# The output projection of a hybrid block: from eight products of halves to seven, with sums of weights made by DMA and by GpSimd

## The chip, the cores and the metric

The kernel runs on one core of a Trainium2 chip. The metric is the device time of one execution in microseconds (us). A core has a matrix engine (TensorE, here PE, with its weight loads shown apart as PEld), VectorE (DVE), ScalarE (ACT), GpSimd (POOL), and SyncE (SP), which only issues DMAs here. Matmuls write into PSUM, which is used as eight banks of 128x512 fp32; everything else is in SBUF.

## The reference

One block over 512 tokens of 1024 features, all in fp32; what matters here is its end:

```python
ya = einsum(ba * conv(ca * xa) * silu(za), w_a_out)          # short convolution branch
yb = einsum(sigmoid(o) * rmsnorm(mlstm(q, k, v, gates)) * silu(zb), w_b_out)   # 2048 -> 1024
merged = sigmoid(ga) * ya + sigmoid(gb) * yb
x = x + einsum('bsd,de->bse', merged, w_o)                   # 1024 -> 1024: the output projection
gate = sigmoid(einsum('bsd,de->bse', rmsnorm(x, g_ple), w_ple_gate))
x = x + gate * (p @ w_ple)
return rmsnorm(x, g_final)
```

## The kernel before

**Products.** Every fp32 product is made of three matmuls on rounded parts (`mm3`, lines 215 to 219): high by high (L217), high by low (L218), low by high (L219). So each operand is cut in two: ACT copies the high part (`whi`, L164) and DVE subtracts it from the original to get the low part (`wlo`, L165). The function `cut` (L221 to L228) does the same with left factors.

**Weights.** A weight block is 512 rows by 512 columns, in a tile `wraw` of 128x4x512 that an SP DMA fills (`load_raw`; four such tiles). It is an *operand* in the list `operands`, used in that order. Its two halves (rows 0 to 255 and 256 to 511, each a tile of 128x1024) are split one at a time by `split_half`; the second half of operand 115 is named `wlo1151`. The split tiles are double-buffered. After the low part of a half, sums that a later operand needs are made in place in another `wraw` tile: on DVE (L169), or by a GpSimd DMA that adds as it writes (L171), 256 or 512 KB each.

**Order of work.** The order on PE, ACT, DVE and POOL is that of the code; nothing is rescheduled. `step` is called after each 12 or 24 matmuls, and calls `tick` (L200), which in this order advances the follow-up work of the step before (`fresh`), splits one weight half of the next operand, and advances the generators in `active` (left factors, loads). So each engine's queue holds what belongs to the last group of matmuls, then a weight half, then left factors.

**Seven products.** `strassen` (L305) multiplies a 2 by 2 arrangement of halves in seven products (a variant of Strassen's scheme), with sums of weight blocks and of left factors as operands. For w_b_out it has two groups (2048 rows), so fourteen *units*, numbered 0 to 13, of 24 matmuls each (two token tiles of four row blocks by three matmuls), with left factors `l0` to `l13` made by `left_heads` (L1045 on) from the tiles `yf`. Its sums are b12 + b22 on DVE for units 7 and 9 and accumulating DMAs for the others. Results go through `sink_heads`: multiply by the gate (`sgx` or `sgb`), add to the merged tile `m`, and, when a pair of token tiles is done, transpose it on PE (`turn_half`, L1095, eight transposes into two banks `pth`) and cut it into the two parts `mg`.

**Output projection.** It is done plainly: two column halves of w_o, each with two row halves and four token tiles, so 8 products of 24 matmuls (operands 114 to 117). The loop at L1179 does the first column half in the order of the transposed quarters; `block_tm` does the second. `add_residual` (L1162) adds a finished bank to x, which lies in `xr`, and squares it on ACT for the norm. Then `turn_to` (L1123) transposes the new x, scales it by g_ple and cuts it into `h2`, the left factor of the w_ple_gate product (operands 118 to 121). `load_end` issues the loads of x, of p @ w_ple (`ple`, computed at the start and kept in DRAM) and of g_final on POOL's queue.

## Time and profile before

| | before |
|---|---|
| median of 3 runs (lowest to highest) | 864.36 us (864.03 to 864.46) |
| profiled execution | 863.96 us, span 862.2 us, mean granted PE clock 0.997 |
| PE busy | 849.0 us, 98%, 4658 instructions |
| PEld | 735.8 us, 85% |
| DVE | 630.4 us, 73% |
| ACT | 483.9 us, 56% |
| POOL | 218.0 us, 25% |

The span runs from the first to the last instruction of the profiled execution; the time beside it has in addition what lies around it, 1.8 us. Busy time is that in which an instruction of the engine runs; matmuls overlap one another, so a busy PE isn't necessarily one at its peak. A row of the listing gives its start in us, its duration, the engine, line and operation, output and inputs by name, their shape, and in brackets the idle time before it with what ended that. In the table by stretch the columns are the stretch, its length, and then the busy time with the count of instructions for PE, PEld, DVE, ACT and POOL, after them the granted clock, the DMA share and GB/s.

### The profile page before, as it was taken

How to read it: one execution, taken by the hardware profiler on the slowest of the kernel's cores; microseconds unless marked ns; L12 is line 12 of the kernel's file. 1: busy time of each engine (PE TensorE's matmuls, PEld its weight loads, DVE VectorE, ACT ScalarE, POOL GpSimd, SP SyncE). 2: the span in 40 equal slices, each digit the busy share in tenths (PEclk: the TensorE clock that was granted, in tenths of full speed). 3: DMA queues.
4: the chain of work that ended last, by engine and by line, in shares of the span. 5: the costliest groups of instructions: out<-in, count | busy, mean ns of one | idle time of the engine just before them, and what ended most of it. 6: DMA issues, size and time to landing. Idle time of an engine off the chain costs nothing.

```text
span 862.2 us, 12152 instructions
## 1 busy us (share of the span) xinstructions
PE 849.0 (98%) x4658; PEld 735.8 (85%) x4658; DVE 630.4 (73%) x813; ACT 483.9 (56%) x702; POOL 218.0 (25%) x221
## 2 busy tenths in 40 slices
PE   9999999999999999999999999999999999999996
PEld 7888888787889988878788999999998888888885
DVE  5786667966767576778568679897986778964465
ACT  7467655657755566565675555545453256634343
POOL 5103222113224322211214323333410212130031
PEclk9999999999999999999999999999999999999998
DMA  9749669589968998775999599899997487884002
GB/s 311 265 135 187 156 133 222 184 235 254 256 135 199 240 224 181 182 183 201 260 243 226 109 243 152 205 175 187 182 346 285 100 196 192 224 319 151 1 1 97
DMA packets 100138, 167.58 MB, mean 194 GB/s; under 512 B 5420, under 2 KB 45920, under 8 KB 98800
## 3 DMA queue, kind: packets, MB, share of 16 engines
q0 software_dynamic: 38672, 70.86, 42.3%
q1 hardware_dynamic: 58544, 90.97, 32.2%
q10 hardware_dynamic: 2864, 4.98, 1.6%
q8 instruction: 36, 0.59, 0.3%
q14 instruction: 22, 0.18, 0.1%
HBM read 150.01 MB, written 16.78 MB: 193 GB/s over the span
## 4 chain that ended last, share of the span: by engine, by line
PE 83%; issue 6%; DVE 4%; DMA 4%; ACT 3%; ACTq 0%; POOL 0%; SPq 0%; POOLq 0%; DVEq 0%
PE mm L218 25%; PE mm L217 25%; PE mm L219 25%; DMA wraw<-in_w_in 2%; DVE wlo L165 1%; PE pv L217 1%; PE pv L218 1%; PE pv L219 1%; ACT whi L164 1%; DMA xin<-in_x 1%; DMA z_d<-c 1%; PE sc L219 1%; PE sc L218 1%; PE sc L217 1%; DVE wraw L169 1%
## 5 line engine op out<-in xcount | busy, mean ns | idle before, releaser
L165 DVE TENSOR_TENSOR wlo<-wraw,whi 128x1024 fp32r<-128x1024 f32 x238 | 298.2, 1256 | 123.0 <-ACT whi L164 121.9
L164 ACT ACTIVATE whi<-wraw 128x1024 fp32r<-128x1024 f32 x240 | 250.8, 1054 | 105.2 <-PE mm L219 45.3
L171 POOL DMA_DIRECT2D wraw<-in_w_in x112 | 136.7, 1416 | 310.0 <-DVE wlo L165 227.1
L333 ACT ACTIVATE s<-mm 128x512 f32<-128x512 f32 x84 | 50.2, 598 | 99.9 <-PE mm L219 97.8
L217 PE MATMUL mm<-whi,hs 128*128 128x512 f32 x256 | 99.9, 390 | 0.0
L218 PE MATMUL mm<-wlo,hs 128*128 128x512 f32 x256 | 99.8, 390 | 0.0
L219 PE MATMUL mm<-whi,hs 128*128 128x512 f32 x256 | 99.7, 389 | 0.0
L217 PE MATMUL mm<-hn_hi,whi 128*128 128x256 f32 (+1 forms) x304 | 93.4, 307 | 0.0
L219 PE MATMUL mm<-hn_hi,wlo 128*128 128x256 f32 (+1 forms) x304 | 93.0, 306 | 0.0
L218 PE MATMUL mm<-hn_lo,whi 128*128 128x256 f32 (+1 forms) x304 | 92.9, 306 | 0.0
L217 PE MATMUL mm<-hs,whi 128*128 128x256 f32 x320 | 90.9, 284 | 0.0
L218 PE MATMUL mm<-hs,whi 128*128 128x256 f32 x320 | 90.5, 283 | 0.0
L219 PE MATMUL mm<-hs,wlo 128*128 128x256 f32 x320 | 90.5, 283 | 0.0
L218 PE MATMUL mm<-wlo,hn_hi 128*128 128x512 f32 x192 | 75.9, 396 | 3.1 <-DVE wlo L165 2.8
L217 PE MATMUL mm<-whi,hn_hi 128*128 128x512 f32 x192 | 75.6, 394 | 0.0
L219 PE MATMUL mm<-whi,hn_lo 128*128 128x512 f32 x192 | 74.9, 390 | 0.0
L218 PEld LDWEIGHTS mm<-hs,whi 128*128 128x128 f32 x320 | 61.4, 192 | 0.0
L217 PEld LDWEIGHTS mm<-hs,whi 128*128 128x128 f32 x320 | 61.4, 192 | 0.0
L219 PEld LDWEIGHTS mm<-hs,wlo 128*128 128x128 f32 x320 | 61.4, 192 | 0.0
L219 PEld LDWEIGHTS mm<-hn_hi,wlo 128*128 128x128 f32 x304 | 58.1, 191 | 2.8 <-POOL wlo L165 0.3
L218 PEld LDWEIGHTS mm<-hn_lo,whi 128*128 128x128 f32 x304 | 58.1, 191 | 2.4
L217 PEld LDWEIGHTS mm<-hn_hi,whi 128*128 128x128 f32 x304 | 58.1, 191 | 2.3
(306 smaller groups left out, 1673.9 us busy)
## 6 DMA issues: line engine op xcount, KB each, us to landing
wraw<-in_w_in SPq DMA_DIRECT2D x32, 1024.0 KB, 5.6
wraw<-in_w_in POOLq DMA_DIRECT2D x52, 512.0 KB, 7.9
wraw<-in_w_in SPq DMA_DIRECT2D x48, 512.0 KB, 5.3
wraw<-in_w_in POOLq DMA_DIRECT2D x60, 256.0 KB, 5.8
wraw<-in_w_b_out SPq DMA_DIRECT2D x7, 1024.0 KB, 6.2
wraw<-in_w_b_out POOLq DMA_DIRECT2D x12, 512.0 KB, 6.6
yt_d<-yc POOLq DMA_DIRECT2D x4, 1024.0 KB, 4.9
wraw<-in_w_a_out SPq DMA_DIRECT2D x4, 1024.0 KB, 6.1
```

What stands on the lines that cost most here:

```text
L164: act.activation(hi, t, AF.Copy)
L165: (e_lo or dve).tensor_tensor(lo, t, hi.bitcast(F32), ALU.subtract)
L169: eng.tensor_tensor(raws[to][:, ks, :], raws[to][:, ks, :], raws[c][:, ks, :], ALU.add)
L171: nc.gpsimd.dma_start(raws[to][:, ks, cs], src[:, ks, :], accum_op=ALU.add)
L217: pe.matmul(ps, lhsT=a[0], rhs=b[0], start=first, stop=False, **kw)
L218: pe.matmul(ps, lhsT=a[0], rhs=b[1], start=False, stop=False, **kw)
L219: pe.matmul(ps, lhsT=a[1], rhs=b[0], start=False, stop=last, **kw)
L333: act.activation(to[i], src, AF.Copy, scale=scale)
```

## The change

The w_o product becomes a seven-product scheme with one group. Its operands are o11, a sum, o21, the next sum, o22, o12 and the last sum. The tile `sums` begins as one more SP load of o11 (rows 512 on, columns 0 to 511), and three pairs of accumulating DMAs on POOL's queue bring it from one sum to the next; a fourth pair adds o22 into o12's tile for its own turn. No left over products are stored: each finished bank, or pair of banks, is added to or subtracted from x at once (`add_residual(row, n, op, src, last)`), and where that was the last part the square and the transposes follow. Banks go on accumulating over products.

The left factors are quarters of the merged tile (256 tokens by 512 features) and sums of them, made by `lefts_1` and `lefts_2` during the last units of the w_b product and by `lefts_3` during the new one. Names: f21, f1 and f11 are plain quarters and sums in fp32, in the place of `yf0` and in two temporaries; `la`, `lb`, `lc`, `ls` hold the cut factors (a11 and s1, s2 and a12, a22, s4 and s3). `at_once=True` lets the sixth w_b task run its sink one step sooner, and the transposes of quarters are issued by those generators. `low_on_pool` puts the low part of the second half of operands 118 (o22) and 119 (o12) on POOL. In the w_b product, the sums b12 + b22 (two pairs of halves) go from DVE to POOL.

After it, x is held with its token tiles in another order (`xs`), `turn_to` works on 256 tokens by 512 features, so `h2` is cut in pieces of 128x256, `ple` is read into the place of `m`, and the first column half of the w_ple_gate product goes over its quarters in the order (0, tokens 2, 3), (1, tokens 2, 3), (1, tokens 0, 1), (0, tokens 0, 1).

The core of the diff:

```diff
-            7: [(b12, b22, 0, dve)], 8: [(b11, b21, 0, None)], 9: [(b12, b22, 1, dve), (b11, b21, 1, None)]}
+            7: [(b12, b22, 0, pool)], 8: [(b11, b21, 0, None)], 9: [(b11, b21, 1, None), (b12, b22, 1, pool)]}
...
+    o11, sums, o21, o22, o12 = (chunk(w_o_v, k, [(n * CW, CW)]) for k, n in ((HC, 0), (HC, 0), (0, 0), (0, 1), (HC, 1)))
+    begun = {sums: o12}
+    first_o = len(operands)
+    operands.extend([(o11, []), (sums, [(sums, o22, None)]), (o21, [(o12, o22, None)]), (sums, [(sums, o21, None)]),
+                     (o22, []), (o12, []), (sums, [])])
+    low_on_pool = {(first_o + i, 1) for i in (4, 5)}
...
-        (e_lo or dve).tensor_tensor(lo, t, hi.bitcast(F32), ALU.subtract)
+        eng = e_lo or (pool if (i, h) in low_on_pool else dve)
+        eng.tensor_tensor(lo, t, hi.bitcast(F32), ALU.subtract)
...
+    def lefts_1():
+        q = quarter_turned(0, 1)
+        yield
+        for ks, pt in q:
+            act.activation(f21[:, ks, :], pt, AF.Copy)
+        q = quarter_turned(0, 0)
+        yield
+        for ks, pt in q:
+            dve.tensor_tensor(f1[:, ks, :], pt, f21[:, ks, :], ALU.subtract)
...
+        cut_quarter(o_a22, q)
+        yield
+        cut(*o_s1, f1)
+
+    def lefts_2():
+        q = quarter_turned(1, 1)
+        yield
+        cut_quarter(o_a11, q)
+        for ks, pt in q:
+            f11.append((ks, temp("c", "f11")))
+            act.activation(f11[-1][1].rearrange("p (f s) -> p f s", f=2), pt, AF.Copy)
+
+    def lefts_3():
+        for ks, f in f11:
+            dve.tensor_tensor(f1[:, ks, :], f1[:, ks, :], f.rearrange("p (f s) -> p f s", f=2), ALU.add)
+        act.activation(o_s2[0], f1, AF.Copy, scale=-1.0)
+        yield
+        dve.scalar_tensor_tensor(o_s2[1], f1, -1.0, o_s2[0].bitcast(F32), ALU.mult, ALU.subtract)
+        q = quarter_turned(1, 0)
+        yield
+        cut_quarter(o_a12, q)
+        for ks, f in f11:
+            pool.tensor_tensor(f21[:, ks, :], f.rearrange("p (f s) -> p f s", f=2), f21[:, ks, :], ALU.subtract)
+        yield
+        for ks, pt in q:
+            dve.tensor_tensor(f1[:, ks, :], f1[:, ks, :], pt, ALU.subtract)
+        yield
+        cut(*o_s4, f1)
+        yield
+        act.activation(o_s3[0], f21, AF.Copy)
+        pool.tensor_tensor(o_s3[1], f21, o_s3[0].bitcast(F32), ALU.subtract)
...
-    strassen(units, sink_heads, groups=2)
+    strassen(units, sink_heads, groups=2, at_once=True)
...
+    for left, banks, tag, row, n, op, last in (
+            (o_a11, acc, order[0], 1, 0, ALU.add, False),
+            (o_s1, cc, order[1], 2, 1, ALU.subtract, False),
+            (o_a12, bb, "x", 1, 0, ALU.add, True),
+            (o_s2, acc, None, 1, 1, ALU.subtract, False),
+            (o_s4, cc, None, 1, 1, ALU.subtract, True),
+            (o_s3, acc, None, 2, 1, ALU.subtract, True),
+            (o_a22, acc, None, 2, 0, ALU.add, True)):
+        w = next_operand()
+        post = add_residual(row, n, op, banks, last)
+        for i in range(2):
...
+            step(post(i))
```

**DVE, last unit of the w_b product.** Between the second low part of unit 12's weights (`wlo1121`) and that of unit 13's (`wlo1131`), before:

```order
L165 TENSOR_TENSOR wlo1121_6992<-wraw61_6171,whi1121_6991 128x1024
L337 TENSOR_TENSOR c_7024<-s_7022,v_6762 128x512
L165 TENSOR_TENSOR wlo1130_7027<-wraw62_6237,whi1130_7026 128x1024
L1029 SCALAR_TENSOR_TENSOR l13_6997<-yf3_6185,l13_6997 128x1024
L225 TENSOR_TENSOR mg1_6495<-pth_7000,mg0_6494 128x2x256
L225 TENSOR_TENSOR mg1_6495<-pth_7001,mg0_6494 128x2x256
L1111 TENSOR_TENSOR sgx0_6345<-sgx0_6345,c_6989 128x512
L1112 TENSOR_TENSOR m_4210<-m_4210,sgx0_6345 128x512
L165 TENSOR_TENSOR wlo1131_7050<-wraw62_6237,whi1131_7049 128x1024
```

and after:

```order
L184 TENSOR_TENSOR wlo1121_6993<-wraw61_6171,whi1121_6992 128x1024
L356 TENSOR_TENSOR c_7029<-s_7027,v_6755 128x512
L1188 TENSOR_TENSOR sgx1_6350<-sgx1_6350,c_7029 128x512
L1189 TENSOR_TENSOR m_4210<-m_4210,sgx1_6350 128x512
L184 TENSOR_TENSOR wlo1130_7034<-wraw62_6240,whi1130_7033 128x1024
L1050 SCALAR_TENSOR_TENSOR l13_6998<-yf3_6188,l13_6998 128x1024
L1149 TENSOR_TENSOR yf0_6185<-pth_7005,yf0_6185 128x512
L1149 TENSOR_TENSOR yf0_6185<-pth_7006,yf0_6185 128x512
L244 TENSOR_TENSOR lc_7040<-pth_7005,lc_7040 128x512
L244 TENSOR_TENSOR lc_7040<-pth_7006,lc_7040 128x512
L184 TENSOR_TENSOR wlo1131_7058<-wraw62_6240,whi1131_7057 128x1024
```

The merge into `m` that stood behind `l13` now stands ahead of it as one of two pairs, and in the place of the two `mg` rows stand the two rows of f1 and the two low parts of a22 (`lc`).

**DVE, middle of the output projection.** From the second low part of one operand over the following ones; before, operand 115, the second of four:

```order
L165 TENSOR_TENSOR wlo1151_7163<-wraw70_6951,whi1151_7162 128x1024
L1165 TENSOR_TENSOR xr_7113<-xr_7113,mm_7124 128x512
L225 TENSOR_TENSOR mg1_6495<-pth_7184,mg0_6494 128x2x256
L225 TENSOR_TENSOR mg1_6495<-pth_7185,mg0_6494 128x2x256
L1165 TENSOR_TENSOR xr_7113<-xr_7113,mm_7149 128x512
L165 TENSOR_TENSOR wlo1160_7244<-wraw71_6995,whi1160_7243 128x1024
L165 TENSOR_TENSOR wlo1161_7261<-wraw71_6995,whi1161_7260 128x1024
L1165 TENSOR_TENSOR xr_7113<-xr_7113,mm_7213 128x512
L1165 TENSOR_TENSOR xr_7113<-xr_7113,mm_7230 128x512
```

and after, operand 116, the third of seven, with product 4's weights (`wlo1170`, `wlo1171`) behind it:

```order
L184 TENSOR_TENSOR wlo1161_7237<-wraw71_6996,whi1161_7236 128x1024
L1178 TENSOR_TENSOR yf0_6185<-yf0_6185,pth_7185 128x512
L1178 TENSOR_TENSOR yf0_6185<-yf0_6185,pth_7186 128x512
L1258 TENSOR_TENSOR xr_7128<-xr_7128,mm_7222 128x512
L184 TENSOR_TENSOR wlo1170_7260<-wraw70_6940,whi1170_7259 128x1024
L244 TENSOR_TENSOR ls_7127<-yf0_6185,ls_7127 128x1024
L1258 TENSOR_TENSOR xr_7128<-xr_7128,mmb_7245 128x512
L184 TENSOR_TENSOR wlo1171_7285<-wraw70_6940,whi1171_7284 128x1024
L1258 TENSOR_TENSOR xr_7128<-xr_7128,mmb_7268 128x512
```

The two `mg` rows are gone, and the rows of sums and cuts of left factors (`yf0`, `ls`) and one more add from a bank to `xr` stand there.

**POOL, the same stage.** Before, its whole queue from the last gate loads to the first use of the norm (a count at the end of a row says that so many like it follow one another):

```order
L1154 DMA xr_7113<-in_x 128x512 x8
L1159 DMA ple_7115<-ple_d_92 128x1024 x4
L1160 DMA gfin_7114<-in_g_final 128x1024
L1200 TENSOR_TENSOR etmp1_7120<-etmp0_7119,mhalf_84 128x4
L1224 TENSOR_TENSOR xg_7443<-xr_7113,gfin_7114 128x512 x4
```

and after, from the sums of f21 to the last load:

```order
L1175 TENSOR_TENSOR yf0_6185<-f11_7095,yf0_6185 128x512
L1175 TENSOR_TENSOR yf0_6185<-f11_7097,yf0_6185 128x512
L158 DMA wraw73_7117<-in_w_o 128x2x512
L158 DMA wraw70_6940<-in_w_o 128x2x512
L1223 DMA ple_7264<-ple_d_92 128x1024
L158 DMA wraw70_6940<-in_w_o 128x2x512
L1223 DMA ple_7264<-ple_d_92 128x1024
L1183 TENSOR_TENSOR ls_7127<-yf0_6185,ls_7127 128x1024
L1223 DMA ple_7264<-ple_d_92 128x1024
L184 TENSOR_TENSOR wlo1181_7326<-wraw72_7061,whi1181_7325 128x1024
L1223 DMA ple_7264<-ple_d_92 128x1024
L1226 DMA gfin_7129<-in_g_final 128x1024
```

Between the loads now stand two sums of quarters, the summing DMAs of w_o, s3's low part and the two low parts of weights (`wlo1181`, `wlo1191`).

## The prediction

> **What bounds the kernel now.** I read, in this order, the page's busy times, the list of what TensorE (PE) waited for, the busy time by stretch, and then each engine's rows in order of time.

> ```profile
> span 862.2 us, 12152 instructions
> PE 849.0 (98%) x4658; PEld 735.8 (85%) x4658; DVE 630.4 (73%) x813; ACT 483.9 (56%) x702; POOL 218.0 (25%) x221
> PE mm L218 <- DVE wlo L165: 2.8, 6, 0.8
> 740.00:766.80 26.80, 26.80 (x128) 22.22 (x127) 26.29 (x31) 14.23 (x18) 7.60 (x15) 1.00 0.72 242
> 766.80:808.00 41.20, 41.20 (x196) 34.35 (x195) 16.10 (x19) 14.61 (x26) 0.47 (x1) 1.00 0.46 168
> 757.16 0.42 PE L218 MATMUL mm<-wlo,l 128*128 128x512 f32 x1
> 757.42 0.40 PE L219 MATMUL mm<-whi,l 128*128 128x512 f32 x1
> 749.39 0.87 PE pth L1102 x8
> ```

> PE is the bound: it waits 2.8 us in all for weights. But from 740.0 to 766.8 VectorE (DVE, third busy figure) works 26.29 of 26.80 us, and only in the output's projection (766.8 to 808) 16.10 of 41.20. So the projection has room; the last units of the product ahead of it have none.

> ```profile
> 746.70 0.60 ACT L333 ACTIVATE s<-mm 128x512 f32<-128x512 f32 x1 [3.02 <-PE mm L219]
> 747.19 1.05 ACT L164 ACTIVATE whi<-wraw 128x1024 fp32r<-128x1024 f32 x1
> 748.14 1.05 ACT L1028 ACTIVATE l<-yf 128x1024 fp32r<-128x1024 f32 x1
> 746.18 1.22 DVE L165 TENSOR_TENSOR wlo<-wraw,whi 128x1024 fp32r<-128x1024 f32 x1
> 747.32 1.22 DVE L1029 SCALAR_TENSOR_TENSOR l<-yf,l 128x1024 fp32r<-128x1024 f32 x1
> 753.28 1.28 DVE L225 TENSOR_TENSOR mg<-pth,mg 128x512 fp32r<-128x512 f32 x2
> 755.80 1.22 DVE L165 TENSOR_TENSOR wlo<-wraw,whi 128x1024 fp32r<-128x1024 f32 x1
> 742.39 0.69 DVE L1111 TENSOR_TENSOR sgb<-sgb,c 128x512 f32<-128x512 f32 x1
> 743.11 0.69 DVE L1112 TENSOR_TENSOR m<-m,sgb 128x512 f32<-128x512 f32 x1
> 743.72 1.22 DVE L165 TENSOR_TENSOR wlo<-wraw,whi 128x1024 fp32r<-128x1024 f32 x1
> 770.35 0.69 DVE L1165 TENSOR_TENSOR xr<-xr,mm 128x512 f32<-128x512 f32 x1 [3.61 <-PE mm L219]
> 771.07 0.63 ACT L1167 ACTIVATE esq<-xr 128x512 f32<-128x512 f32 x1 [7.31 <-DVE xr L1165]
> 771.70 1.07 ACT L224 ACTIVATE mg<-pth 128x512 fp32r<-128x512 f32 x2
> ```

> Prices, as steps from one start to the next: DVE 1.14 for 1024 columns (1.22 until its reader may start), 0.60 for 512 (0.69; 0.72 where the next row needs the result: 742.39 to 743.11); ScalarE (ACT) 0.95 (1.05), 0.50 (0.60), 0.63 for a square; 0.04 to hand over to another engine (770.35 + 0.69 to 771.07). PE: 757.16 to 757.42 holds a wait; an undisturbed step is (749.39 − 683.04 − 0.87) / 288 = 0.227, since 24 stretches of 12 matmuls and one set of 8 transposes lie between the row below and that of 749.39.

> ```profile
> 683.04 0.39 PE L217 MATMUL mm<-whi,l 128*128 128x512 f32 x1
> ```

> **The gain.** One product of halves less is 24 matmuls: 24 × 0.227 = 5.44 us. The eight sets of transposes stay eight.

> **The new waits.** In the new loop PE needs a fresh weight half every 5.44 us, 6.31 where a set of transposes (0.87) comes between. Each second half passes ACT (high part), then DVE or GpSimd (low part), in queues that also hold the adds from the banks and the left factors. What counts is the chain from the end of one late low part to the end of the next; PE waits for what it has over 5.44 or 6.31. GpSimd's part needs its own rows:

> ```profile
> 18.35 2.40 POOL L165 TENSOR_TENSOR wlo<-wraw,whi 128x1024 fp32r<-128x1024 f32 x1 [2.18 <-ACT whi L164]
> 19.20 2.07 DVE L228 SCALAR_TENSOR_TENSOR hn_lo<-pt,prm,hn_hi 128x512 fp32r<-128x512 f32 x3 [1.01 <-ACT hn_hi L227]
> 22.79 0.19 DVE L631 TENSOR_TENSOR wg<-wg_raw,wg 128x32 fp32r<-128x32 f32 x1
> 22.90 2.45 POOL L165 TENSOR_TENSOR wlo<-wraw,whi 128x1024 fp32r<-128x1024 f32 x1 [2.16 <-ACT whi L164]
> 23.10 2.30 DVE L631 TENSOR_TENSOR wg<-wg_raw,wg 128x32 fp32r<-128x32 f32 x1
> 829.61 1.29 POOL L1224 TENSOR_TENSOR xg<-xr,gfin 128x512 f32<-128x512 f32 x1 [1.36 <-DVE xr L1215]
> 834.74 3.44 DVE L165 TENSOR_TENSOR wlo<-wraw,whi 128x1024 fp32r<-128x1024 f32 x2
> 834.90 2.20 POOL L1224 TENSOR_TENSOR xg<-xr,gfin 128x512 f32<-128x512 f32 x1 [1.35 <-DVE xr L1215]
> L171 POOL DMA_DIRECT2D wraw<-in_w_b_out x12 | 14.5, 1215 | 68.9 <-DVE wlo L165 68.9
> L1159 POOL DMA_DIRECT2D ple<-ple_d x4 | 2.1, 534 | 1.3 <-DMA xr<-in_x 1.0 <-issue 0.3
> ```

> A GpSimd sum of 1024 columns takes 2.42. DVE rows with both inputs in SBUF stop for it (0.19 becomes 2.30 at 23.10), rows that read a bank don't (0.69 each at 19.20), and GpSimd stops for DVE's (1.29 becomes 2.20). I take it that the two take turns whole. [...]

> (a) The four weight sums (two pairs of halves) leave DVE: 4 × 1.14 = 4.56 us of DVE are freed where PE did not wait, so nothing is gained. But l7's low part, which followed one sum on DVE, now stands behind both turns of GpSimd's first pair: laid end to end, the first turn ends 0.16 before unit 7's predecessor is half done, then come a weight's low part (1.14), the second turn (2.35) and l7's own 1.22 = 4.71, while PE has 12 matmuls and wants it at the third of unit 7: 0.16 + 2.72 + 0.45 = 3.3. Late by 1.4.
> (b) Last unit: its second low part stood 9.62 us behind the row of 746.18 (755.80) and was just in time. Ahead of it now: one more pair sgx and m (0.72 + 0.60), two bank reads for f1 in the place of the two mg rows, and lc's two low parts (1.20), which wait for ACT (0.16 for its copy of a bank that DVE must have read first, 0.35 for the high part queued behind the copies): 0.72 + 0.60 + 1.20 + 0.51 = 3.0. Two more sets of transposes give PE 1.74. Late by 1.3.
> (c) Product 1: 1.14 low part, 1.14 s1's, 1.14 first half, 0.60 + 0.73 a11's, 0.50 copy, 1.09 high, = 6.34: 0.9 over 5.44.
> (d) Product 2: 1.14, 0.72 + 0.60 merge, 1.14, 0.60 + 0.73 sums of f1, 0.95 s2's high, 1.09 = 6.97: 0.65 over 6.31.
> (e) Product 3: 1.14, 1.14 s2's low, 0.60 add, 1.14, 1.20 a12's, 0.60 add = 5.82, and 0.92 behind GpSimd's first half of f21: 1.3 over 5.44.
> (f) Product 4: 1.14, 1.20 f1, 0.60 add, 1.14, 1.14 s4's low, 0.73 add, 0.63 square, 1.09 = 7.67: 2.2 over 5.44.
> (g) Product 5, low part on GpSimd: 0.04, issue of a summing DMA 1.20, ple's 0.53, s3's low 2.35, DVE's turn 1.14, 2.42 = 7.68: 1.35 over 6.31.
> (h) Product 6, again on GpSimd: 1.14, four cuts of h2 1.76 with the wait for ACT between them, 0.73 add, 0.63 square, 1.09, 2.42 = 7.77: 2.3 over 5.44.
> (i) Product 7 is in time (its chain has 5.0 of 6.31). First half of the next weights: 1.14, h2 1.77, 0.72, 0.63, 1.09, 1.22 = 6.57 against 2.72 + 0.87 + 1.59 (seven matmuls): 1.4. (j) Second: 0.73, 0.63, 1.09, 1.14, h2 with ACT 1.24, 1.09, 1.22, less 0.08 that the ends overlap = 7.06: 0.75 over 6.31.

> Sum: 1.4 + 1.3 + 0.9 + 0.65 + 1.3 + 2.2 + 1.35 + 2.3 + 1.4 + 0.75 = 13.55. Net 13.55 − 5.44 = +8.1.

> The unknown price is the h2 cut of 128x256 on DVE and ACT:

> ```profile
> 791.45 1.41 DVE L228 SCALAR_TENSOR_TENSOR h<-ptk,prm,h 128x512 fp32r<-128x512 f32 x2 [1.75 <-ACT h L227]
> 93.59 0.42 DVE L864 SCALAR_TENSOR_TENSOR pp<-sc,e 128x256 f32<-128x256 f32 x1
> wraw<-in_w_b_out POOLq DMA_DIRECT2D x12, 512.0 KB, 6.6
> xr<-in_x POOLq DMA_DIRECT2D x8, 256.0 KB, 5.4
> ```

> Between 0.33 (93.59 to the next start) and 0.70 (half of the 1.41 for two of 512) for one; I take 0.38, the row of 256 columns with 0.05 more for a bank as input. The four in each of (h), (i) and (j) move the sum by −0.6 to +3.8. Transfers: eight summing DMAs of 512 KB on GpSimd's queue and one more load on SP's are new. Product 4's first half is the tightest: the issue follows product 2's first low part (1.20), 6.6 to land, while its high part comes 7.2 later but its low part only 13; so up to 5 us of lateness stays hidden. Summing DMAs that queue behind GpSimd's sums start up to 2.4 later, nine ahead of use, and SP's next load waits for the same sums, with twenty to go: nothing. The second pair of x pieces goes behind a summing DMA (1.20 + 0.53 + 5.4 after product 2's first low part) and is wanted 8.5 after it: hidden by 1.4. ple, now read into m's place, is wanted 40 us on. DVE's own 3% and the hand-over (0.03 to 0.06) move the sum by −2 to +1.5, since they enter ten chains.

> **Rivals.** First, GpSimd runs beside DVE: then (a) is nothing, (e) loses 0.92, (g) 0.65 and (h) 1.45, since GpSimd waits for no turn and DVE starts (h) sooner: 9.1 of waits, +3.7, 867.6 us. The row of 23.10 speaks against it. Second, on the other side, the change does what it removes and nothing is late, because queued engines run further ahead than I let them: 863.96 − 5.44 = 858.5 us. It decides where the ten chains stay under 5.44 or 6.31; for it speaks that 766.8 to 808 shows DVE at 39% and that PE waited only 2.8 us before; against it the row of 757.16, where DVE was already just in time, and (f), which is over by 2.2 without GpSimd at all. Third, waits of about 5.4 in all cancel the gain: every chain would have to be 0.8 shorter: 864 us. Fourth, PE's clock falls in the pauses, or summing DMAs land over 5 us late: above 875.9. The granted clock is 1.00 beside the 0.8 us wait and lower only at the end:

> ```profile
> 150.00:210.00 60.00, 58.44 (x260) 46.74 (x259) 45.62 (x49) 38.86 (x54) 10.14 (x11) 1.00 0.76 225
> 840.00:862.20 22.20, 14.01 (x85) 12.41 (x83) 12.40 (x33) 7.32 (x17) 2.19 (x4) 0.88 0.25 94
> ```

> No row has a 2 us pause amid work; a fall would add from nothing to a few us. [...]

> **How the numbers follow.** The profiled execution took 863.96 us (span 862.2), 0.4 under the median of 864.36. 863.96 + 8.1 = 872.1. Chances: this case 0.62, first rival 0.20, second 0.08, third 0.04, fourth 0.06. Range: below, the first rival with chains 1.3 shorter in sum, 866.3; above, the long h2 cut, 875.9. It leaves out the second, third and fourth and a little of the others' edges. A difference of 0.2% (1.7 us) is about what can be told from none: faster 0.08, same 0.05, slower 0.87.

> **What would show it.** PE's matmuls 24 fewer; PE waits on wlo, in the last unit and the seven products, of 0.6 to 2.3 us each, about 13 in all (2.8 before); GpSimd's wlo and sums at 2.4 or more, DVE rows stretched beside them. Wrong if PE has no waits from 740 on (then 858.5), or if DVE's rows keep 1.22 beside GpSimd's sums (then 867.6).

## The result, and the profile after

The changed kernel takes 878.01 us (median of 4 runs, 876.71 to 878.77), the one before 864.41 us (median of 4): 1.0152 times as long, 95% interval 1.0133 to 1.0171. The prediction was 872.1 us, with a range up to 875.9: the sign was right, the size and the range were not. The profiled execution took 876.71 us, the fastest of the four.

The page, first lines:

```profile
span 874.9 us, 12195 instructions
PE 850.4 (97%) x4634; PEld 731.9 (84%) x4634; DVE 654.9 (75%) x834; ACT 495.8 (57%) x722; POOL 249.3 (28%) x238
```

PE has 24 matmuls fewer, and yet its busy time is 1.4 us longer than before: some of them ran slowly. The list of what PE waited for (total, times, longest):

```profile
PE mm L237 <- DVE wlo L184: 9.3, 14, 3.2
PE mmb L237 <- DVE wlo L184: 1.8, 1, 1.8
PE mm L238 <- DVE l L1050: 1.6, 1, 1.6
PE mm L236 <- ACT whi L182: 0.5, 1, 0.5
PE mm L237 <- POOL wlo L184: 0.2, 1, 0.2
```

About 13.4 us of waits for operands, where one row of 2.8 us stood. The 2.8 us, and 2.7 of the 13.4, lie ahead of 600 us, in stages that the change doesn't touch; from there on it is 10.7 us after and nothing before. PE's rows with the longer waits in order of time (the bracket is the wait; rows between them are left out):

```profile
723.24 0.50 PE L238 MATMUL mm<-whi,l 128*128 128x512 f32 x1 [1.61 <-DVE l L1050]
761.85 0.50 PE L237 MATMUL mm<-wlo,l 128*128 128x512 f32 x1 [0.77 <-DVE wlo L184]
782.73 0.50 PE L237 MATMUL mmb<-wlo,lb 128*128 128x512 f32 x1 [1.83 <-DVE wlo L184]
790.35 0.50 PE L237 MATMUL mm<-wlo,lb 128*128 128x512 f32 x1 [0.28 <-DVE wlo L184]
798.81 0.50 PE L237 MATMUL mm<-wlo,ls 128*128 128x512 f32 x1 [3.15 <-DVE wlo L184]
807.77 0.50 PE L237 MATMUL mm<-wlo,ls 128*128 128x512 f32 x1 [0.23 <-POOL wlo L184]
822.32 0.50 PE L237 MATMUL mm<-wlo,h 128*128 128x512 f32 x1 [0.76 <-DVE wlo L184]
```

They are the left factor of unit 7, the last unit, products 3 to 6 and the first weights of w_ple_gate. The longest, before product 5 (798.81), is explained by DVE's and POOL's rows of the same time:

```profile
716.35 5.75 POOL L188 TENSOR_TENSOR wraws<-wraws,wraw 128x1024 f32<-128x1024 f32 x2 [3.36 <-DMA wraws<-in_w_b_out]
717.35 2.48 DVE L184 TENSOR_TENSOR wlo<-wraw,whi 128x1024 fp32r<-128x1024 f32 x1 [1.50 <-ACT whi L182]
719.76 3.42 DVE L1050 SCALAR_TENSOR_TENSOR l<-yf,l 128x1024 fp32r<-128x1024 f32 x1
...
779.07 4.73 POOL L1175 TENSOR_TENSOR yf<-f,yf 128x512 f32<-128x512 f32 x2
779.64 3.03 DVE L184 TENSOR_TENSOR wlo<-wraw,whi 128x1024 fp32r<-128x1024 f32 x1
...
791.90 2.88 POOL L1183 TENSOR_TENSOR ls<-yf,ls 128x1024 fp32r<-128x1024 f32 x1
792.63 6.12 DVE L184 TENSOR_TENSOR wlo<-wraw,whi 128x1024 fp32r<-128x1024 f32 x1 [1.74 <-ACT whi L182]
794.88 2.78 POOL L184 TENSOR_TENSOR wlo<-wraw,whi 128x1024 fp32r<-128x1024 f32 x1
```

DVE's row of 1.22 us took 6.12: it began under GpSimd's low part of s3, and ended 1.1 after the next GpSimd row (794.88 + 2.78 = 797.66, against 798.75). Between the two it got no turn, though 0.1 us lay between their rows. Under the two sums at 716.35 it did: 2.48 and 3.42 us, one sum each. So it did, by the records one by one, under the two sums of f21 at 779.07: the first ended at 781.48, DVE's row at 782.67, the second sum at 783.79.

What PE lost besides waits shows in the busy times by stretch of 3.4 us (PE, PEld, DVE, ACT, POOL, then the granted clock):

```profile
779.90:783.30 3.40, 1.57 (x8) 0.98 (x7) 3.40 (x3) 0.00 (x0) 3.40 (x4) 1.00 0.80 204
783.30:786.70 3.40, 3.40 (x9) 2.65 (x8) 3.40 (x5) 1.06 (x1) 2.49 (x4) 0.50 1.09 259
...
796.90:800.30 3.40, 1.49 (x6) 1.24 (x7) 3.40 (x4) 0.00 (x0) 1.76 (x3) 1.00 1.08 302
800.30:803.70 3.40, 3.40 (x10) 2.63 (x9) 3.04 (x6) 1.04 (x3) 0.00 (x0) 0.51 1.02 416
```

After the waits of 1.83 and 3.15 us, PE ran 3.4 us at half clock each time: steps of 0.427 us where 0.227 is usual, some 1.6 us lost twice.

In what follows "lost" is the sum, over the matmuls from 600 us on, of what a step from one start to the next has over 0.227 us (waits, the step of 0.34 that follows each, slow steps). It is 0 before and 17.7 us after, 3.2 of it slow steps. 863.96 − 5.44 + 17.7 = 876.2 against the 876.71 of the profiled execution: the saving and the lost time are all but 0.5 us of the result.

### The profile page after: what moved, and what is told of

Same layout as the page of the kernel before. It is cut to its first block, busy times and chain, and to the rows that moved or that the text cites. A ratio compares the mean times of both kernels' runs of the same rounds, so it can differ in the third digit from the quotient of the medians.

```text
span 874.9 us, 12195 instructions
## 1 busy us (share of the span) xinstructions
PE 850.4 (97%) x4634; PEld 731.9 (84%) x4634; DVE 654.9 (75%) x834; ACT 495.8 (57%) x722; POOL 249.3 (28%) x238
## 4 chain that ended last, share of the span: by engine, by line
PE 74%; DVE 8%; issue 8%; ACT 5%; DMA 4%; ACTq 0%; POOL 0%; SPq 0%; POOLq 0%; DVEq 0%
PE mm L237 23%; PE mm L238 22%; PE mm L236 22%; DVE wlo L184 3%; ACT whi L182 2%; DMA wraw<-in_w_in 2%; PE pv L236 1%; PE pv L238 1%; PE pv L237 1%; DMA xin<-in_x 1%; DVE xr L1258 1%; DMA z_d<-c 1%; PE sc L238 1%; PE sc L237 1%; PE sc L236 1%
## 5 line engine op out<-in xcount | busy, mean ns | idle before, releaser
L184 DVE TENSOR_TENSOR wlo<-wraw,whi 128x1024 fp32r<-128x1024 f32 x242 | 314.0, 1299 | 129.2 <-ACT whi L182 128.7
L182 ACT ACTIVATE whi<-wraw 128x1024 fp32r<-128x1024 f32 x246 | 256.7, 1053 | 104.6 <-PE mm L238 43.5
## 6 DMA issues: line engine op xcount, KB each, us to landing
wraw<-in_w_in POOLq DMA_DIRECT2D x52, 512.0 KB, 8.2
wraw<-in_w_in SPq DMA_DIRECT2D x48, 512.0 KB, 5.2
wraw<-in_w_in POOLq DMA_DIRECT2D x60, 256.0 KB, 5.9
wraw<-in_w_b_out POOLq DMA_DIRECT2D x12, 512.0 KB, 6.0
```

The costliest lines, as they stand in the source:

```text
L182: act.activation(hi, t, AF.Copy)
L184: eng.tensor_tensor(lo, t, hi.bitcast(F32), ALU.subtract)
```

## The experiments

Two theories at first. *Turns*: waits come from GpSimd's rows, behind which DVE stands, and from the order of the queues. *Queue*: DVE simply has too much to do, whoever does the sums.

**Only the four sums of w_b back on DVE.**

```diff
-  7: [(b12, b22, 0, pool)] ... (b12, b22, 1, pool)
+  7: [(b12, b22, 0, dve)] ... (b12, b22, 1, dve)
```

> The changed kernel with the four sums b12 + b22 back on DVE; all else stays. Theory (turns): the 1.9 us wait on l7 at 723 and the 0.6 us wait in unit 10 come from the two engines taking turns, so both go and nothing new is late: about 2.4 us less than the changed kernel, near 875.6. Rival (queue): DVE's queue is the limit whatever GpSimd does; 4.56 us more of rows on DVE then give no gain, 878 or later, and waits of the same size in units 7 to 10.

874.74 us, ratio to before 1.0123 (1.0109 to 1.0137). The waits in units 7 and 10 are gone, lost time 15.2 us (2.5 less). DVE did more and the kernel was faster, which speaks for the turns.

**The same part in the kernel before: the four sums on GpSimd.**

```diff
-  7: [(b12, b22, 0, dve)] ... 9: [(b12, b22, 1, dve), (b11, b21, 1, None)]
+  7: [(b12, b22, 0, pool)] ... 9: [(b11, b21, 1, None), (b12, b22, 1, pool)]
```

> The kernel before with one part of the change alone: the four sums b12 + b22 on GpSimd. Theory (turns): l7's low part or its weights stand behind GpSimd's turns, 1.7 to 2.5 us slower than before, 866.1 to 866.9. Rival (GpSimd beside DVE costs nothing): 864.4.

867.34 us, 1.0038 (1.0025 to 1.0051): 2.9 us slower, a little more than expected. Its list of PE's waits has the new row for the left factor, and more for the weights:

```profile
PE mm L218 <- DVE wlo L165: 3.9, 8, 0.9
PE mm L219 <- DVE l L1029: 0.9, 1, 0.9
```

This part alone is a loss.

**Everything that GpSimd got back on DVE.** The sums as above, and

```diff
-    low_on_pool = {(first_o + i, 1) for i in (4, 5)}
+    low_on_pool = set()
-            pool.tensor_tensor(f21[:, ks, :], ...
+            dve.tensor_tensor(f21[:, ks, :], ...
-        pool.tensor_tensor(o_s3[1], f21, ...
+        dve.tensor_tensor(o_s3[1], f21, ...
```

> The changed kernel with every sum and every low part that GpSimd got back on DVE (b12 + b22, f21, s3's low part, the low parts of the second halves of o22 and o12). GpSimd then only issues DMAs there. Theory (turns): waits that are left come from the order of the queues, 12.6 us in all against 17.7, none above 1.6 us, so no stretch with PE at half clock: 864.4 + 7.2 = 871.6. Rival (queue): about 13 us of rows more on DVE make every later chain longer: 878 to 885.

872.60 us, 1.0093 (1.0079 to 1.0106), lost 12.9 us. 5.4 us faster than the change, with nine more rows on DVE: the queue theory falls. The nine rows are about 9 us at DVE's prices, not the 13 of the expectation, and DVE's busy time even fell, from 654.9 to 647.9 us, since no row stands behind GpSimd's. One miss: there was still a slow stretch (789.4 to 792.8), after two waits of about 1 us close together in product 4.

**As that, with late squares.**

```diff
             dve.tensor_tensor(sl, sl, src[i], op)
             if last:
+                if (row, n) != (2, 0):
+                    yield
                 sq = temp("c", "esq")
```

> As the one with everything on DVE, but in the output projection the square of a finished piece of x (ACT) is queued one step later, except in the last product. Theory: ACT's square waits for DVE's add, which waits for PE, and the next weights' high part stands behind it; without that, the waits of product 4 shrink from 2.2 to 0.4 and those of products 5 to 7 and of the first w_ple_gate weights go: 864.4 - 0.7 = 863.7. Rival (DVE's amount of work, not the order, is the limit): as the one with everything on DVE, within 1 us.

864.65 us, 1.0000 (0.9991 to 1.0009), lost 5.4 us; 1 us above the expected 863.7. No engine does less than with everything on DVE. The squares stand one step later in ACT's queue, the transposes and h2 cuts that follow a square move with it, and 8 us are gone, 1.6 of them the slow stretch. ACT's rows with everything on DVE, ahead of product 4's second half:

```profile
785.74 0.63 ACT L1261 ACTIVATE esq<-xr 128x512 f32<-128x512 f32 x1 [2.40 <-DVE xr L1258]
786.37 1.04 ACT L182 ACTIVATE whi<-wraw 128x1024 fp32r<-128x1024 f32 x1
```

and with late squares:

```profile
785.23 1.04 ACT L182 ACTIVATE whi<-wraw 128x1024 fp32r<-128x1024 f32 x1
786.17 0.61 ACT L1263 ACTIVATE esq<-xr 128x512 f32<-128x512 f32 x1
```

In the first, ACT stands idle for 2.40 us before the square, which waits for DVE's add, which waits for PE's bank; the weights that PE needs next stand behind it.

**Late squares alone, on the change as it was.** The same diff.

> The changed kernel with the late squares alone; everything that GpSimd got stays with it. Theory (two causes that add up): the waits of products 4 and 6 and of the w_ple_gate weights shrink, those behind GpSimd (unit 7, products 3 and 5) stay, with the slow clock behind the longest: 869 to 873. Rival (the squares were all of it): 864.7, as with everything on DVE.

870.84 us, 1.0077 (1.0062 to 1.0091), lost 11.4 us. So the two causes nearly add up: of the 13.4 us between the change and late squares on DVE, 7.2 go with the order alone and 5.4 with GpSimd's work alone.

**Only the two low parts of weights back on DVE.** The `low_on_pool` line alone.

> The changed kernel with only the low parts of the second halves of o22 and o12 back on DVE; the four sums b12 + b22, f21 and s3's low part stay on GpSimd. Theory (in product 5 one DVE row stood behind two GpSimd rows): the first low part of o22 then stands behind s3's alone, about 3 us instead of 6.1, and the wait at product 5 falls from 3.4 to under 1.5, with no slow stretch of PE behind it; in return the order's waits of products 6 and 7 come back (1.6 and 0.9): 873 to 876. Rival (the long row has another cause than the second GpSimd row): it stays at 6 us and the time at 878.

876.83 us, 1.0141 (1.0125 to 1.0156). The long row, now with one GpSimd row ahead of it:

```profile
793.22 2.88 POOL L1183 TENSOR_TENSOR ls<-yf,ls 128x1024 fp32r<-128x1024 f32 x1
793.95 3.24 DVE L184 TENSOR_TENSOR wlo<-wraw,whi 128x1024 fp32r<-128x1024 f32 x1 [1.74 <-ACT whi L182]
```

3.24 us instead of 6.12, PE's loss at product 5 0.6 instead of 3.5, and no slow stretch there: the second GpSimd row was the cause. The time is 0.8 above the range expected, since product 3's loss grew to 3.3 and the returning wait of the w_ple_gate weights (2.6) brought a slow stretch of its own.

**Pauses put into the kernel before.**

```diff
-        (e_lo or dve).tensor_tensor(lo, t, hi.bitcast(F32), ALU.subtract)
+        for _ in range(1 + MORE.get((i, h), 0)):
+            (e_lo or dve).tensor_tensor(lo, t, hi.bitcast(F32), ALU.subtract)
```

> The kernel before, with DVE's low part of the second half of operands 115 to 119 written 3, 6, 8, 7 and 5 times more (the same subtraction again, 1.14 us each), so that PE pauses in its last stages, by about 1.7, 3.1, 2.8, 5.3 and 1.9 us. Only PE's clock after each pause is of interest, not the time. Theory (stretches): the clock is set for each stretch of 3.4 us by how long PE worked in the stretch before, half speed when under about half: one or two slow stretches of 3.4 us after the pause of 5.3, one after those of 2.8 and 3.1 unless a border cuts them in two equal pieces, none after 1.7, and after 1.9 only if it lies in one stretch; slow stretches lie on one grid of 3.4 us. Rival (one long pause): only a pause of over 3.4 us slows the clock, so only that of 5.3. Rival (length alone): every pause over 2 us does, at once, wherever it lies.

One run, of 879.79 us. The pauses came out as 1.6, 3.2, 2.6, 3.6 and 0.5 us. By stretches of 3.41 us, laid so that one begins about where a slow one does (by the clock's records the slow ones begin at 807.50 and 824.57):

```profile
787.14:790.55 3.41, 1.44 (x7) 0.86 (x5) 3.31 (x4) 0.00 (x0) 0.00 (x0) 1.00 0.00 0
790.55:793.97 3.42, 2.39 (x10) 1.99 (x11) 2.17 (x3) 1.81 (x5) 0.00 (x0) 1.00 0.36 75
...
804.21:807.62 3.41, 0.96 (x4) 0.48 (x3) 3.34 (x5) 0.00 (x0) 0.00 (x0) 0.98 0.01 2
807.62:811.03 3.41, 3.41 (x10) 2.67 (x9) 3.41 (x6) 0.00 (x0) 0.00 (x0) 0.52 0.80 270
...
821.27:824.69 3.42, 1.53 (x6) 1.24 (x7) 3.39 (x5) 0.89 (x3) 0.00 (x0) 0.98 0.00 0
824.69:828.10 3.41, 3.41 (x10) 2.66 (x9) 1.58 (x3) 2.95 (x6) 0.00 (x0) 0.52 0.00 0
```

The pauses of 2.6 and 3.6 were followed by 3.4 us at half clock, that of 3.2 was not, nor that of 1.6. Length alone doesn't decide, and over 3.4 us isn't needed: both rivals fall. Both slow stretches lie on one grid (17.1 us apart, five times 3.41), as the theory has it; but the stretch from 787.14, with PE busy for 1.44 of 3.41, should have been followed by a slow one and wasn't. Most of this is a matter of where the borders are put. With stretches that end 0.2 us ahead of each possible change of the clock, a shift found by trying on these traces, it has 1.76:

```profile
786.82:790.23 3.41, 1.76 (x8) 1.13 (x6) 3.34 (x3) 0.00 (x0) 0.00 (x0) 1.00 0.00 0
720.72:724.13 3.41, 1.58 (x7) 1.03 (x6) 3.41 (x2) 2.59 (x3) 1.98 (x1) 1.00 0.11 10
721.64:725.05 3.41, 1.81 (x8) 1.45 (x9) 3.41 (x3) 1.57 (x2) 0.46 (x1) 1.00 0.50 136
```

The second row holds the wait on l7 with late squares alone, behind which a slow stretch began at 724.34; the third holds the same wait in the change, behind which none did. Laid so, in all fourteen traces, the twelve slow stretches amid the matmuls have PE busy for 0.43 to 1.81 us ahead of them, and every other stretch has 1.76 or more. So in these traces about half of a stretch (1.71) separates the two, within 0.1 us. The ends of matmuls are modelled, and no run was made to test the shift.

**Order, and the sums by DMA.** On top of late squares: `None` for `dve` in the four sums, the second pair one unit earlier; a22's cut out of the last unit; s2's cut a step later.

```diff
-        cut_quarter(o_a22, q)
         yield
         cut(*o_s1, f1)
+        q22.extend(q)                      # cut at the end of lefts_2
...
+        yield
         act.activation(o_s2[0], f1, AF.Copy, scale=-1.0)
-        yield
-        dve.scalar_tensor_tensor(o_s2[1], ...)
         q = quarter_turned(1, 0)
         yield
         cut_quarter(o_a12, q)
+        dve.scalar_tensor_tensor(o_s2[1], ...)
```

> The one with late squares, with three things more: the four sums b12 + b22 by accumulating DMAs instead of DVE (issued one unit earlier for the second pair), a22's cut after that of s1 and a11 instead of in the last unit of w_b, and s2's cut one step later. Theory (order): the waits in unit 10, in the last unit and of product 2 go or shrink to 0.3, those of products 1, 3 and 4 stay at 0.6, 1.6 and 0.4, so 864.4 - 2.5 = 861.9. Rival (summing DMAs land late, or DVE's amount is the limit): 864 to 868, with PE waiting in units 10 to 12.

863.07 us, 0.9980 (0.9971 to 0.9988); the profiled execution took 861.55, lost 3.3 us. The waits expected to go went, and it is faster than before, by less than expected in the median.

**f21 by an accumulating DMA from SBUF to SBUF.**

```diff
-            dve.tensor_tensor(f21[:, ks, :], f..., f21[:, ks, :], ALU.subtract)
+            nc.gpsimd.dma_start(f21[:, ks, :], f..., accum_op=ALU.add)
```

> The one before it (order, sums by DMA), with f21 -> f11 - f21 also by an accumulating DMA (f21 is stored negated, so that it is an addition) and s3's cut two steps later. It takes 1.2 us of DVE from product 3. Theory: product 3's wait falls from 1.6 to 0.4, nothing new is late: 861.1. Rival (the DMA from SBUF to SBUF on GpSimd's queue holds up the summing DMAs of the weights behind it): a wait on whi or wlo in products 4 to 7, 863 or more.

867.57 us, 1.0036 (1.0022 to 1.0049): the rival's time. ACT waited for the sum, and later for the summing DMA of weights:

```profile
790.34 1.06 ACT L1188 ACTIVATE ls<-yf 128x1024 fp32r<-128x1024 f32 x1 [7.16 <-DMA yf<-f]
803.14 1.06 ACT L182 ACTIVATE whi<-wraw 128x1024 fp32r<-128x1024 f32 x1 [3.51 <-DMA wraw<-in_w_o]
```

The two transfers of 256 KB, issued at 775.2 to 777.5, were awaited until 790.3. The second wait isn't shown to be theirs: it is as long in the next run (3.85 us), which has no such transfer.

**f21 on DVE, three steps later.**

```diff
-        for ks, f in f11:                  # behind a12's cut
-            dve.tensor_tensor(f21[:, ks, :], ...)
...
+        for ks, f in f11:                  # behind s4's cut
+            dve.tensor_tensor(f21[:, ks, :], ...)
+        yield
         act.activation(o_s3[0], f21, AF.Copy)
```

> The one with order and sums by DMA, with f21's two rows on DVE (1.2 us) moved three steps later, ahead of s3's cut, which comes one step later. Theory (order): product 3's wait falls from 1.5 to 0.4 and product 5 gets one of 0.4: waits of 3.3 become 2.3, so 1.0 less than that one, 862.1 if it repeats its median of 863.1. Rival (the waits only move on): the same time within 0.4.

862.58 us, 0.9983 (0.9973 to 0.9993). Against the one without it the difference is 0.5, too little to tell. Product 3's loss fell from 1.5 to 0.6 as expected, but product 7 lost 1.6 for weights that came late.

**The same with the sums on DVE.** `dve` for `None` in the four sums, in the units that the change gives them.

> The one before it with the four sums b12 + b22 on DVE again instead of by DMA, so with no byte more read than the changed kernel reads. Theory (order): DVE has room for them there once the last unit is lighter, except for a wait of 0.4 in unit 10 as with late squares; the transfers that are saved don't matter: 862.5. Rival (the sums by DMA were what made the gain): 864 or more, with waits in units 7 to 13.

863.35 us, 0.9993 (0.9984 to 1.0002), lost 4.4 us: between the two theories. The sums by DMA are at most a part of the gain.

**ple later.** The loads of ple, and that of g_final behind them, six steps later.

```diff
-        yield
+        for _ in range(6):
+            yield
         u = mp.tile([P, NT, D], F32, name="ple", tag="m")
```

> The one with f21 later (sums by DMA), with the four loads of ple (512 KB each) and that of g_final issued six steps later. There the second half of the last sum's weights came late: ACT's high part at 799.73 had waited 3.85 us for the summing DMA, and PE 1.6 us, while ple's loads and four weight blocks were in flight. Theory (transfers collide): without ple's 2 MB ahead of it the sum lands in time, the 1.6 us wait goes: 862.6 - 1.5 = 861.1. Rival (the weight blocks of w_ple_gate alone fill the DMA engines): the wait stays above 1 us, 862.2 or more.

861.61 us, 0.9970 (0.9959 to 0.9980), lost 2.6 us: 2.6 us faster than the kernel before, 16.4 faster than the change, and the fastest here. ACT's row for product 7's second half with f21 later:

```profile
799.73 1.06 ACT L182 ACTIVATE whi<-wraw 128x1024 fp32r<-128x1024 f32 x1 [3.85 <-DMA wraw<-in_w_o]
```

and with ple later:

```profile
797.21 1.06 ACT L182 ACTIVATE whi<-wraw 128x1024 fp32r<-128x1024 f32 x1 [1.26 <-PE mm L238]
```

The summing DMA is in time, and what is left of PE's waits there is short:

```profile
PE mm L237 <- DVE wlo L184: 3.3, 7, 0.8
PE mmb L237 <- DVE wlo L184: 0.7, 1, 0.7
```

## Why the prediction was right and wrong

What PE lost in the profiled execution, by the prediction's terms (us):

| term | predicted | lost |
|---|---|---|
| (a) unit 7 | 1.4 | 1.9 |
| unit 10 | none | 0.6 |
| (b) last unit | 1.3 | 1.4 |
| (c), (d) products 1, 2 | 1.55 | 1.4 |
| (e) product 3, slow steps after it | 1.3 | 2.1 + 1.6 |
| (f) product 4 | 2.2 | 0.6 |
| (g) product 5, slow steps after it | 1.35 | 3.5 + 1.6 |
| (h) product 6 | 2.3 | 0.5 |
| (i), (j) first w_ple_gate weights | 2.15 | 2.5 |
| sum | 13.55 | 17.7 |

- **The gain** was right: in each kernel with the seven products, the time of the profiled execution is 863.96 − 5.44 + what PE lost, within 1.5 us (late squares: 863.96 against 865.45; ple later: 861.1 against 861.73).
- **The places of the waits** were right but for (g), which came at DVE's low part of product 5's first half and not at GpSimd's of the second; one more, in unit 10 behind GpSimd's second pair of sums, was missing: the prediction followed the first pair only.
- **The step that failed first is "the two take turns whole"**, in (g). It was the author's estimate, from rows in which DVE met one GpSimd row (0.19 becomes 2.30 at 23.10). That DVE stops for GpSimd held (6.12 us for a row of 1.22). That it gets its turn after one GpSimd row held in unit 7 and in product 3, but not in product 5, where it stood behind two; (g) measured 3.5 us instead of 1.35. Only the low parts on DVE shows the second row as the cause. In (e) the turn was right and a size was off: the first row of f21 took 2.41 us on GpSimd (779.07 to 781.48), so that DVE's stood 1.8 behind it and not 0.92, and (e) measured 2.1 instead of 1.3. Why a row of 512 columns took 2.41 there stays open.
- **The second, and larger, is the clock**, left out of the sum and counted as a rival of 0.06 together with late transfers, "from nothing to a few us", a guess with no row behind it: it took 3.2 us. Its case was put low since the profile before has no pause of 2 us amid work; in the change a wait of 1.83 us was enough. Length alone is not the condition: of the pauses put in, one of 2.6 us was followed by a slow stretch and one of 3.2 was not. PE worked in 1.57 of the 3.40 us ahead of a slow stretch here, the two slow stretches with the pauses are 17.1 us apart (five times 3.41), and what fits them is PE busy for less than about half of a stretch.
- **(f) and (h) came out small** since PE ran slowly beside them, not since their chains were short. Product 4's late low part ended 7.63 us after product 3's (782.67 to 790.30), as the 7.67 of (f) had it, but 1.6 us of that went on PE's slow steps. For (h), DVE's late row ended at 798.75 and GpSimd's next low part at 807.72, 8.97 us later: the 7.77 predicted and 1.2 for two adds that had stood behind the long row. Against it PE had 5.44, six more matmuls (1.36), since the wait ahead had come at the first half of product 5, and 1.6 us of slow steps.

```profile
789.07 1.23 DVE L184 TENSOR_TENSOR wlo<-wraw,whi 128x1024 fp32r<-128x1024 f32 x1 [1.74 <-ACT whi L182]
801.01 0.86 DVE L247 SCALAR_TENSOR_TENSOR h<-ptk,prm,h 128x256 fp32r<-128x256 f32 x2
805.28 2.44 POOL L184 TENSOR_TENSOR wlo<-wraw,whi 128x1024 fp32r<-128x1024 f32 x1 [6.62 <-ACT whi L182]
```

- **Luck.** Without the slow steps the terms sum to 14.5, near the 13.55 predicted, but by errors that cancel: (e) and (g) were 2.95 too small, (f) and (h) 3.4 too large.
- **The h2 cut**, the price taken between rows: 0.86 us for two of 128x256 (DVE's row at 801.01 above), against the 2 × 0.38 taken: near enough to change nothing.
- **The rivals.** GpSimd beside DVE (867.6) is refuted by the two runs with the four sums alone. "Nothing is late" is refuted for this order, and nearly reached in another: with ple later PE loses 2.6 us. What the prediction didn't ask is whether the waits belong to the seven products or to the order in which they were written. Late squares answers it: 5.44 saved, 5.4 lost.

The range ended at 875.9 with the long h2 cut alone above the sum; DVE standing behind more than one GpSimd row was not in it, and the clock was left above it, where the time then fell. Medians add 1 us, as the profiled execution of the change was the fastest of its four.

## What to carry to other kernels

When a faster algorithm hands work to engines with room, write out each in-order queue and ask what stands behind an instruction that waits: here squares that waited for the bound engine's own result ahead of that engine's next weights cost 8 us with everything on DVE, slow clock included, more than the saving of 5.44. Work given to GpSimd isn't free because GpSimd is idle: here DVE stood behind one or two of its rows with two SBUF inputs, and rows of 1.22 us took 2.48 to 6.12. And count on PE's clock as well: where waits left PE busy for 1.57 and 1.49 of 3.40 us, it was granted 0.50 for the next 3.4.

## What the runs showed of the hardware that was not expected

```profile
yf<-f POOLq DMA_DIRECT2D x2, 256.0 KB, 13.7
wraw<-in_w_o POOLq DMA_DIRECT2D x5, 512.0 KB, 14.9
wraw<-in_w_b_out POOLq DMA_DIRECT2D x14, 512.0 KB, 7.7
```
